# A hybrid layer on one core: a 20th ring slot, one adaLN accumulator instead of two, and other orders of the loads and the weight rounding

## The chip, the cores and the metric

The kernel runs on one core of a Trainium2 chip. The metric is the device time of one execution in microseconds (us). Before the change three runs took 653.33, 655.2 and 656.99 us; their median is 655.2 us.

## The reference

The layer takes x (256 tokens of 1024 values, float32) and a conditioning vector c. Cut to what matters:

```python
mod = silu(c) @ w_ada + b_ada                       # six sections of 1024 columns
shift1, scale1, gate1, shift2, scale2, gate2 = split(mod, 6)
hn   = rms_norm(x, g1) * (1 + scale1) + shift1
proj = hn @ w_in                                    # 3592 columns
q_m, k_m, v_m, o_m, gates(8), q_a, k_a, v_a = split(proj)
q_m, k_m = split(silu(causal_conv4(concat(q_m, k_m))))
h_m = rms_norm(mlstm(q_m, k_m, v_m, gates)) * sigmoid(o_m)     # 4 heads x 128
h_a = causal_attention(q_a, k_a, v_a)                          # 8 heads x 64
x   = x + gate1 * (concat(h_m, h_a) @ w_out)
hn2 = rms_norm(x, g2) * (1 + scale2) + shift2
ffn = top-1 of 4 groups, top-2 of its 8 experts:
      sum of weight * ((silu(hn2 @ w_gate[e]) * (hn2 @ w_up[e])) @ w_down[e])
out = rms_norm(x + gate2 * ffn, g_final)
```

The weights of all 32 experts (three matrices of 1024 by 512 each) are read, 6 loads of 1 MiB per expert.

## The kernel before, in words

*Weights and the ring.* Every large weight comes in loads of about 1 MiB on the SP queue into a pool `ring` of `RING = 19` slots of `SLOT = 4 * 520` float32 columns. A slot is free again when its last reader is done, so the SP queue waits for that reader before it issues the load that reuses the slot. `x`, its normalised and transposed copies and the activations `hH`, `hL` lie in ring slots too. The names of loads are: `B0` to `B3` (tile `wb`) for section 1 of adaLN (scale1), `A00` to `A53` (tile `wa`) for two k-chunks each of sections 0, 2, 3, 4, 5, then `ga0` to `om1` (tiles `wi_ga`, `wi_ka`, ...) for four k-chunks each of a 512-column group of `w_in`, and `W0` to `W3` (`wo`) for `w_out`. The string `LOADS` gives their order on SP. Behind them come the experts (`load_expert`, L1206: `we` for gate and up, `wd` for down).

*The projections.* There are 72 steps: seven column groups in the order ga, ka, va, qm, km, vm, om with eight k-chunks each are steps 0 to 55; `w_out` is steps 56 to 71. A float32 product is made of three products in a faster format: in `split` (L390) ACT rounds a weight chunk to `wh` (L398) and DVE or POOL makes the residual `wl` (L399; POOL for the steps in `ON_POOL_L`). `step` (L407) then issues the matmuls of `wh` with `hH`, of `wh` with `hL` and of `wl` with `hH` (L432 where the result is wanted transposed, L403 to L405 elsewhere). The four buffers `NB = 4` of `wh` and `wl` let the rounding run some steps ahead. `hH` and `hL` are the rounded activations and their residual, first scaled only (`h_scaled`), for va and later with shift (`h_full`, L467 to L469).

*adaLN.* A section is a vector times a 1024 by 1024 matrix. Section 1 is done on TensorE (`scale1`, L291). In the others DVE multiplies k-chunks by their scalar and sums them into an accumulator `acc` of 128 by 1024 (`ada_dve`, L219: all eight chunks of section 2, six in sections 0, 3, 4 and 5), and TensorE does the remaining chunks and sums the accumulator over its partitions (`ada_mm`, L227). The accumulators are two buffers of the pool `wk`; `y4`, the results of four experts that wait for their outer product, have the same tag and so the same buffers. `shift_cols` (L453) turns section 0 into the columns `sh`, through the table `dd`. `shift_bias` (L457) multiplies them with the weights of q and k.

*What sets the order.* TensorE's order is written out by hand from `PLAN`, a table that gives each piece of side work a step before which it stands (`ad5:64` is section 5's matmuls before step 64). The other engines' orders come from a scheduler, which takes the pieces as `PLAN` places them; `AFTER` adds constraints: `w42>dec0` says that the piece `dec0` is issued behind the rounding of step 42 on the engines that both use. Loads on SP are issued in the order of `LOADS`, each as soon as its slot is free.

*Gates.* The eight gate columns of `w_in` lie beside group ga, whose tiles are 520 columns wide for them; POOL copies them out into `wg` (`gate_w`, L573). The scan over tokens runs between `gate_cum` (`pf`, L600) and the decays (`dec0` to `dec3`).

*Experts.* Tokens are gathered per expert by a one-hot matmul (`pair`, L969), then L1094 makes gate and up, L1111 down, `evac_y` (L1116) multiplies by gate2 into `y4`, and after every fourth expert an outer product (`acc_mm`) adds `y4` to the output. An overflow part, entered only where an expert has more than 32 tokens, does the rest in single blocks.

Of the kernel before, what the change touches and what calls it, by code (L numbers as in the profile page):

```python
# [42 lines left out]
PLAN = """
    shb:7 scl:24 hs0:-3 hs1:-3 sb1:1 hs2:1 hs3:1 sb2:3 hs4:3 hs5:3 sb3:4 hs6:4 hs7:4 a00:4 a01:4 a02:6 a03:6 a04:9
    a05:9 a24:20 a25:20 a26:22 a27:23 a44:39 a45:40 a46:41 a47:42 a34:53 a35:54 a36:55 a37:56 a54:62 a55:63 a56:64
    a57:64 ldga0:-3 ldga1:-3 ldA00:-3 ldA01:-3 ldA02:-3 ldA03:-3 ldka0:-3 ldka1:-3 ldva0:-3 ldva1:-3 ldqm0:-3 ldqm1:2
    ldkm0:7 ldkm1:15 ldvm0:12 ldvm1:17 ldA20:-3 ldom0:19 ldom1:20 ldA21:4 ldA22:5 ldA23:5 ldA40:15 ldW2:21 ldW3:37
    ldA41:19 ldA42:19 ldW0:41 ldW1:42 ldA43:21 ldA30:33 ldA31:40 ldA32:41 ldA33:45 ldA50:49 ldA51:51 ldA52:53 ldA53:53
    gw0:5 gw1:6 ad0:11 shc:13 sbq:14 sbk:18 hf0:13 hf1:13 hf2:13 hf3:13 hf4:14 hf5:14 hf6:16 hf7:16 eq0:10 eq1:10
    eq2:10 eq3:10 bq0:17 bq1:17 bq2:17 bq3:17 ek0:20 ek1:18 ek2:18 ek3:18 eva0:24 eva1:24 vm1:33 gp0:18 gp1:20 glog:20  # L50
    gcum:23 grow:26 gcol:33 gs0:26 gs1:26 gs2:26 gs3:27 gs4:27 gs5:27 gs6:28 gs7:28 mo:28 mr:30 dec0:40 dec1:41
    dec2:45 dec3:46 am0:20 ae0:20 ap0:23 av0:25 ae1:20 ap1:24 av1:26 am2:22 ae2:22 ap2:25 av2:26 ae3:22 ap3:26 av3:28
# [20 lines left out]
def tile_hymba_layer(  # L73
# [1057 lines left out]
    def overflow():  # L1131
        n = nc.values_load(nblk_i[0:1, 0:1], min_val=0, max_val=MAXB - 1)
        wb = [wk.tile([P, 512], F32, name=f"wov{i}", tag=("wh", "wl")[i % 2], bufs=NB) for i in range(4)]
        with tc.If(n > 0):
# [251 lines left out]
```

## Time and profile before

| | |
|---|---|
| median of three runs | 655.2 us (653.33 to 656.99) |
| the profiled execution | 657.88 us, span 656.2 us |
| TensorE busy | 522.0 us (80% of the span) |
| VectorE, ScalarE, GpSimd busy | 248.9, 130.8, 73.6 us |
| moved by DMA | 250.43 MB, 380 GB/s over the span |
| longest line | L1094 (gate and up of the experts), 153.7 us of TensorE |

The profiled execution is one of the slower ones of this kernel; its trace gives the durations, the runs give the time. The page cuts the span into 40 slices of 16.4 us. The first eleven or twelve hold the mixer, all later ones the experts. Busy shares are an average over both, so they are read by slice or by stretch.

### The profile page before, as it was taken

The numbers are of one execution on the slowest core, as the hardware profiler recorded it, in microseconds if no ns is written. First come the engines' busy times: TensorE is split into PE (matmuls) and PEld (weight loads), VectorE is DVE, ScalarE is ACT, GpSimd is POOL, SyncE is SP. The second block draws the span as 40 slices with busy tenths as digits, with TensorE's granted clock in tenths as the row PEclk, the third lists the DMA queues.
The fourth block names the chain that finished last, engine by engine and source line by source line (L and its number), as shares of the span: only waits on it lengthen the run. The fifth ranks groups of instructions, "written<-read, shape, count | busy, mean of one in ns | idle before, by whom it ended". The sixth has DMA issues, their size and how long they took to land. (4 is left out here: it accounts for less than half of the span.)

```text
span 656.2 us, 16271 instructions
## 1 busy us (share of the span) xinstructions
PE 522.0 (80%) x7198; PEld 385.4 (59%) x7198; DVE 248.9 (38%) x604; ACT 130.8 (20%) x296; POOL 73.6 (11%) x94
## 2 busy tenths in 40 slices
PE   3879899998998888777677697858876797774885
PEld 3768699786876756545455563635463555452754
DVE  3598799998662322212121212122121312121122
ACT  5343856855440000000000000000000000000023
POOL 7131244724001000000000000000000000000000
PEclk9798999998979999988698866988696977779598
DMA  9999978599969999999999999999999999999982
GB/s 270 380 393 400 395 298 302 212 370 420 379 218 393 415 414 416 415 419 414 417 415 416 416 417 415 416 417 416 418 413 417 415 416 417 417 415 415 416 340 104
DMA packets 56522, 250.43 MB, mean 382 GB/s; under 512 B 4424, under 2 KB 8672, under 8 KB 40064
## 3 DMA queue, kind: packets, MB, share of 16 engines
q1 hardware_dynamic: 55328, 247.51, 94.4%
q0 software_dynamic: 1024, 1.81, 1.1%
q8 instruction: 58, 0.95, 0.6%
q14 instruction: 16, 0.13, 0.1%
q10 hardware_dynamic: 96, 0.03, 0.0%
HBM read 248.27 MB, written 1.06 MB: 380 GB/s over the span
## 5 line engine op out<-in xcount | busy, mean ns | idle before, releaser
L1094 PE MATMUL pgu<-we,xg 128*32 128x128 f32 x4096 | 153.7, 300 | 58.6 <-DMA we<-in_w_expert_up_dram 26.9
L1094 PEld LDWEIGHTS pgu<-we,xg 128*32 128x32 f32 x4096 | 124.0, 120 | 99.8 <-issue 49.7
L1111 PE MATMUL py<-wd,ht 128*32 128x256 f32 x992 | 80.0, 460 | 28.6 <-DVE ht L1105 17.9
L1101 DVE TENSOR_TENSOR hm<-sg,pgu 128x128 f32<-128x128 f32 x32 | 9.2, 288 | 216.6 <-ACT sg L1099 216.6
L1116 DVE TENSOR_TENSOR y<-py,gate 32x256 f32<-32x256 f32 x124 | 52.1, 420 | 92.5 <-PE py L1111 91.2
L1099 ACT ACTIVATE sg<-pgu 128x128 f32<-128x128 f32 x32 | 8.9, 277 | 391.5 <-PE pgu L1094 385.5
L969 PE MATMUL pgx<-oh,xn 128*128 128x64 f32 x512 | 72.3, 303 | 0.8 <-DVE oh L952 0.8
L969 PEld LDWEIGHTS pgx<-oh,xn 128*128 128x128 f32 x512 | 68.1, 215 | 7.0 <-issue 7.0
L1111 PEld LDWEIGHTS py<-wd,ht 128*32 128x32 f32 x992 | 31.3, 125 | 61.1 <-DVE ht L1105 24.3
L225 DVE SCALAR_TENSOR_TENSOR acc<-wa,csil,acc 128x1024 f32<-128x1024 f32 x27 | 38.5, 1426 | 0.2
L912 PE MATMUL acc<-y,owt 128*128 128x512 f32 x64 | 38.0, 722 | 0.1
L959 POOL TENSOR_TENSOR ow<-oh,gg 128x128 f32<-128x128 f32 x16 | 5.9, 394 | 209.4 <-PE pw L1122 183.7
L973 DVE TENSOR_TENSOR xg<-pgx,s 128x256 f32<-128x256 f32 x32 | 12.2, 419 | 37.2 <-PE pgx L969 34.7
L1103 PE MATMUL ph<-ident,hm 128*128 128x128 f32 x32 | 11.1, 346 | 15.9 <-DVE hm L1101 15.1
L1287 POOL MEMSET owz<- 128x1024 f32 x1 | 1.0, 952 | 197.8 <-PE pgu L1094 197.8
L912 PEld LDWEIGHTS acc<-y,owt 128*128 128x128 f32 x64 | 12.9, 226 | 14.0 <-issue 13.5
L1103 PEld LDWEIGHTS ph<-ident,hm 128*128 128x128 f32 x32 | 5.4, 168 | 23.1 <-DVE hm L1101 23.1
L432 PE MATMUL pka<-hH,wl 128*128 128x256 f32 x32 | 9.7, 304 | 5.0 <-DVE wl L399 3.6
L403 PE MATMUL po<-wh,hTH 128*128 128x512 f32 x32 | 13.6, 426 | 0.0
L432 PE MATMUL pga<-hH,wh 128*128 128x256 f32 x32 | 10.4, 324 | 3.9 <-ACT hH L442 3.8
L405 PE MATMUL po<-wh,hTL 128*128 128x512 f32 x32 | 13.2, 413 | 0.0
L404 PE MATMUL po<-wl,hTH 128*128 128x512 f32 x32 | 13.2, 413 | 0.0
(365 smaller groups left out, 764.4 us busy)
## 6 DMA issues: line engine op xcount, KB each, us to landing
we<-in_w_expert_gate_dram SPq DMA_DIRECT2D x64, 1024.0 KB, 20.0
we<-in_w_expert_up_dram SPq DMA_DIRECT2D x64, 1024.0 KB, 20.0
wd<-in_w_expert_down_dram SPq DMA_DIRECT2D x63, 1024.0 KB, 20.0
wa<-in_w_ada_dram SPq DMA_DIRECT2D x20, 1024.0 KB, 11.5
wb<-in_w_ada_dram SPq DMA_DIRECT2D x4, 1024.0 KB, 11.9
wo<-in_w_out_dram SPq DMA_DIRECT2D x4, 1024.0 KB, 7.8
wi_ka<-in_w_in_dram SPq DMA_DIRECT2D x2, 1024.0 KB, 16.2
wi_va<-in_w_in_dram SPq DMA_DIRECT2D x2, 1024.0 KB, 18.2
```

The lines of the kernel that those rows point to most:

```text
L225: V.scalar_tensor_tensor(ACC[sec], w, csil[:, kc:kc + 1], ACC[sec], op0=ALU.mult, op1=ALU.add)
L403: T.matmul(p, aH, bH, start=first, stop=False)
L404: T.matmul(p, aH, bL, start=False, stop=False)
L405: T.matmul(p, aL, bH, start=False, stop=last)
L432: T.matmul(o, a[:, cs], b[:, kc, :], start=(kc == 0 and i == 0 and fb % 2 == 0), stop=(kc == KC - 1 and i == 2), skip_group_check=True)
L912: T.matmul(acc2[tb, h][:, cols], lhsT, rhs, start=start, stop=stop, skip_group_check=True)
L969: T.matmul(pj[j], xn2[:, tb, j, :], oh(tb), start=(tb == 0), stop=(tb == NT - 1))
L973: V.tensor_tensor(xg[:, js], src, s2[:, js].unsqueeze(2).to_broadcast([P, 4, n]), op=ALU.mult)
L1094: T.matmul(pgu[32 * g:32 * g + 32, u * P:(u + 1) * P], xg[:, j, :], wt[:, g * P:(g + 1) * P], start=j == 0 and u == 0, stop=j == KC - 1, s ...
L1103: T.transpose(ph, hm, ident)
L1111: T.matmul(py[32 * g:32 * g + 32, :], ht[:, 32 * f:32 * f + 32], wt[:, c0:c0 + S], start=first, stop=last, skip_group_check=True)
L1116: V.tensor_tensor(y4[r0:r0 + 32, g * S:(g + 1) * S], py[32 * g:32 * g + 32, :], gate2[r0:r0 + 32, g * S:(g + 1) * S], op=ALU.mult)
```

## The change

The ring gets a 20th slot and each slot 24 columns fewer (2056). The room comes from the second accumulator (`acc`, `y4` and the others of that tag now have one buffer), from `dd`, which now lies in columns of `gate2`, from `emt` and `nq`, which now lie in `la` and `lf`, and from the gate columns of group ga, which are loaded by two small DMAs on ACT's queue straight into `wg`. In the final part g_final's row is loaded into row 0 of `gfin`. The overflow part writes its block into a weight slot. `LOADS`, `PLAN`, `AFTER` and `ON_POOL_L` are changed; of `PLAN` two lines are shown.

```diff
-RING = 19
-SLOT = 4 * 520
+RING = 20
+SLOT = 2056
 LOADS = """
-    ga0 B1 B2 ga1 B3 A01 A00 ka0 A02 A03 ka1 va0 va1 qm0 A20 qm1 A21 A22 ...
-    W2 A30 W3 A31 W0 A32 W1 A33 A50 A51 A52 A53
+    ga0 B1 B2 B3 ga1 A01 A00 ka0 A02 ka1 A03 va0 va1 qm0 qm1 A20 A21 A22 ...
+    W2 W3 A30 A31 W0 A32 W1 A33 A50 A51 A52 A53
 PLAN = """
...
-    gcum:23 grow:26 gcol:33 ...
+    gcum:22 grow:26 gcol:33 ...
...
-    ad3:58 sc3:58 ad5:64 tri:40 ... a50:58 a51:59 a52:60 a53:61 ...
+    ad3:58 sc3:58 ad5:68 tri:40 ... a50:56 a51:57 a52:58 a53:59 ...
 AFTER = """
-    w42>dec0 w42>dec1 w47>dec2 w47>dec3
+    w42>dec0 w42>dec1 w47>dec2 w47>dec3 w15>eq0 w8>a03 sb0>w1 sb0>w2
-ON_POOL_L = {2, 5, 8, 11, 14, 17, 20, 23, 26, 27, 31, 33, 37, ...}
+ON_POOL_L = {5, 8, 11, 14, 17, 20, 23, 27, 28, 31, 33, 37, ...}
...
-            acc = ACC[sec] = wk.tile([P, D], F32, name=f"acc{sec}", tag="acc")
+            acc = ACC[sec] = wk.tile([P, D], F32, name=f"acc{sec}", tag="acc", bufs=1)
...
-    dd = const([P, KC, 33], "dd")
+    dd = gate2[:, 0:KC * 33].rearrange("p (j n) -> p j n", j=KC)
...
-    CH = {"ga": (2048, 520, True), "ka": (2568, 512, True), ...
+    CH = {"ga": (2056, 512, True), "ka": (2568, 512, True), ...
...
-    emt = const([P, NT, MH], "emt")
+    emt = la
...
     def gate_w(h):
-        G.tensor_copy(wg[:, 4 * h:4 * h + 4, 0:8], WI["ga", h][:, :, 0:8])
+        A.dma_start(wg[:, 4 * h:4 * h + 4, 0:8], w_in[0, h * 512:(h + 1) * 512, 2048:2056]
+                    .rearrange("(k p) n -> p k n", p=P))
...
-    nq = const([P, NT, MH], "nq")
+    nq = lf
...
-                y1 = wk.tile([P, D], F32, name="y_ov", tag="acc")
-                evac_y(y1, py, 0)
+                for g in range(4):
+                    V.tensor_tensor(wb[g // 2][0:SL, g % 2 * S:(g % 2 + 1) * S], py[32 * g:32 * g + 32, :],
+                                    gate2[0:SL, g * S:(g + 1) * S], op=ALU.mult)
...
-            grow = wk.tile([1, D], F32, name="grow", tag="acc")
-            G.dma_start(grow, g_final.unsqueeze(0))
+            G.dma_start(gfin[0:1, :], g_final.unsqueeze(0))
...
-            y4 = wk.tile([P, D], F32, name=f"y4_{e}", tag="acc")
+            y4 = wk.tile([P, D], F32, name=f"y4_{e}", tag="acc", bufs=1)
```

SP's queue, from the second half of the scale weights on. Before, `wi_ga_248` is ga1 between `wb` loads, and `wi_ka_262` is ka1 behind `wa_3_260`, which is A03:

```order
L286 DMA wb_246<-in_w_ada_dram 128x8x256
L374 DMA wi_ga_248<-in_w_in_dram 128x4x520
L286 DMA wb_250<-in_w_ada_dram 128x8x256
L206 DMA wa_1_252<-in_w_ada_dram 128x2x1024
L206 DMA wa_0_254<-in_w_ada_dram 128x2x1024
L374 DMA wi_ka_256<-in_w_in_dram 128x4x512
L206 DMA wa_2_258<-in_w_ada_dram 128x2x1024
L206 DMA wa_3_260<-in_w_ada_dram 128x2x1024
L374 DMA wi_ka_262<-in_w_in_dram 128x4x512
```

The same place now:

```order
L286 DMA wb_243<-in_w_ada_dram 128x8x256
L286 DMA wb_245<-in_w_ada_dram 128x8x256
L374 DMA wi_ga_247<-in_w_in_dram 128x4x512
L206 DMA wa_1_249<-in_w_ada_dram 128x2x1024
L206 DMA wa_0_251<-in_w_ada_dram 128x2x1024
L374 DMA wi_ka_253<-in_w_in_dram 128x4x512
L206 DMA wa_2_255<-in_w_ada_dram 128x2x1024
L374 DMA wi_ka_257<-in_w_in_dram 128x4x512
L206 DMA wa_3_259<-in_w_ada_dram 128x2x1024
```

ga1 moved behind the last `wb` load, and ka1 ahead of A03.

VectorE in steps 8 to 16, around the shift columns. Before, `wl_577`, `wl_598` and `wl_645` are the residuals of steps 12, 13 and 15:

```order
L225 SCALAR_TENSOR_TENSOR acc_478<-wa_1_252,csil,acc_478 128x1024 x2
L399 TENSOR_TENSOR wl_522<-wi_ka_256,wh_521 128x512
L399 TENSOR_TENSOR wl_541<-wi_ka_256,wh_540 128x512
L225 SCALAR_TENSOR_TENSOR acc_478<-wa_2_258,csil,acc_478 128x1024 x2
L277 TENSOR_TENSOR dd<-pa_613,m_100 128x8x32
L279 TENSOR_REDUCE sh_217<-dd 128x8
L455 COPY shb<-sh_217 128x256
L467 TENSOR_SCALAR xnT<-xnT,s_125,sh_217 128x256 x8
L399 TENSOR_TENSOR wl_577<-wi_ka_262,wh_576 128x512
L399 TENSOR_TENSOR wl_598<-wi_ka_262,wh_597 128x512
L399 TENSOR_TENSOR wl_645<-wi_ka_262,wh_644 128x512
```

Now, where `gate_113` is the table `dd` in its new place and `wl_576`, `wl_594`, `wl_639` are steps 12, 13 and 15:

```order
L399 TENSOR_TENSOR wl_521<-wi_ka_253,wh_520 128x512
L225 SCALAR_TENSOR_TENSOR acc_477<-wa_1_249,csil,acc_477 128x1024
L399 TENSOR_TENSOR wl_540<-wi_ka_253,wh_539 128x512
L225 SCALAR_TENSOR_TENSOR acc_477<-wa_2_255,csil,acc_477 128x1024 x2
L399 TENSOR_TENSOR wl_576<-wi_ka_257,wh_575 128x512
L399 TENSOR_TENSOR wl_594<-wi_ka_257,wh_593 128x512
L277 TENSOR_TENSOR gate_113<-pa_609,m_100 128x8x32
L279 TENSOR_REDUCE sh_216<-gate_113 128x8
L455 COPY shb<-sh_216 128x256
L467 TENSOR_SCALAR xnT<-xnT,s_125,sh_216 128x256 x8
L399 TENSOR_TENSOR wl_639<-wi_ka_257,wh_638 128x512
```

The residuals of steps 12 and 13 moved ahead of the shift columns and of the eight `xnT` operations, that of step 15 stayed behind them.

VectorE in the output projection, from the gating of `hh` on. Before, `wl_1843`, `wl_1875` and `wl_1912` are the residuals of steps 62, 64 and 66:

```order
L703 TENSOR_TENSOR hh<-hh,so_1794 128x512
L248 TENSOR_TENSOR d_1822<-pa_1809,m_100 128x256
L250 TENSOR_REDUCE sh_235<-d_1822 128x8
L737 TENSOR_TENSOR sh_235<-sh_235,colp 128x8
L728 TENSOR_TENSOR wrs<-wst,sh_235 128x8x4
L728 TENSOR_TENSOR wrs<-wst,sh_235 128x8x32
L399 TENSOR_TENSOR wl_1843<-wo_1391,wh_1842 128x512
L739 TENSOR_REDUCE cbs<-wrs 128x36
L728 TENSOR_TENSOR wrs<-wst,s_234 128x8x4
L728 TENSOR_TENSOR wrs<-wst,s_234 128x8x32
L399 TENSOR_TENSOR wl_1875<-wo_1496,wh_1874 128x512
```

The same place now, with `acc_1775` the accumulator of section 5 and `wl_1842`, `wl_1874` the residuals of steps 62 and 64:

```order
L704 TENSOR_TENSOR hh<-hh,so_1793 128x512
L223 TENSOR_SCALAR acc_1775<-wa_0_1549,csil 128x1024
L248 TENSOR_TENSOR d_1821<-pa_1808,m_100 128x256
L225 SCALAR_TENSOR_TENSOR acc_1775<-wa_0_1549,csil,acc_1775 128x1024
L250 TENSOR_REDUCE sh_232<-d_1821 128x8
L399 TENSOR_TENSOR wl_1842<-wo_930,wh_1841 128x512
L225 SCALAR_TENSOR_TENSOR acc_1775<-wa_1_1607,csil,acc_1775 128x1024
L738 TENSOR_TENSOR sh_232<-sh_232,colp 128x8
L399 TENSOR_TENSOR wl_1874<-wo_1454,wh_1873 128x512
L719 SCALAR_TENSOR_TENSOR hTL<-ht_1867,col,hTH 128x256
L225 SCALAR_TENSOR_TENSOR acc_1775<-wa_1_1607,csil,acc_1775 128x1024
L729 TENSOR_TENSOR wrs<-wst,sh_232 128x8x4
```

Section 5's six operations stand between the last residuals of the output projection, whose place before was ahead of all of this, where section 3's six stand now.

## Rows read from the trace of the kernel before

**Rows 1.** The page, 40 slices of the span: share (tenths) and rate of the DMA engines.

```profile
DMA  9999978599969999999999999999999999999982
GB/s 270 380 393 400 395 298 302 212 370 420 379 218 393 415 414 416 415 419 414 417 415 416 416 417 415 416 417 416 418 413 417 415 416 417 417 415 415 416 340 104
```

**Rows 2.** The chain that ended last: start us, us, what it spent them on.

```profile
623.51 21.05 DMA wd<-in_w_expert_down_dram
```

**Rows 3.** Timeline of SP, 181 to 196: start us, us, engine, line, operation.

```profile
181.80 3.91 SPq L1216 DMA_DIRECT2D wd<-in_w_expert_down_dram  x2
195.22 0.34 SPq L1211 DMA_DIRECT2D we<-in_w_expert_gate_dram  x1
```

**Rows 4.** Waits of SP's queue, 168 to 206: us in total, times, longest.

```profile
SPq L1211 <- PE pgu L1094: 12.2, 6, 9.4
```

**Rows 5.** Windows: us, busy PE, PEld, DVE, ACT, POOL, clock, DMA share, GB/s.

```profile
188.00:192.00 4.00, 4.00 (x21) 4.00 (x20) 0.98 (x3) 0.00 (x0) 0.00 (x0) 0.50 0.61 242
192.00:196.00 4.00, 4.00 (x61) 3.76 (x63) 2.58 (x15) 1.06 (x3) 0.00 (x0) 0.50 0.01 2
```

**Rows 6.** Waits of TensorE, 120 to 172.

```profile
PE ht L715 <- DVE hh L703: 2.0, 2, 1.3
PE pm L675 <- DVE st L665: 0.6, 1, 0.6
```

**Rows 7.** Waits of TensorE, 36 to 60.

```profile
PE pka L432 <- DVE wl L399: 3.6, 1, 3.6
PE pka L432 <- POOL wl L399: 1.4, 1, 1.4
```

**Rows 8.** Timeline of VectorE, 45 to 51.

```profile
45.39 3.62 DVE L467 TENSOR_SCALAR xnT<-xnT,s,sh 128x256 f32<-128x256 f32 x8
48.94 1.88 DVE L399 TENSOR_TENSOR wl<-wi_ka,wh 128x512 fp32r<-128x512 f32 x3
```

**Rows 9.** Windows behind three waits of TensorE.

```profile
48.00:52.00 4.00, 2.33 (x16) 2.33 (x17) 4.00 (x11) 1.17 (x3) 0.00 (x0) 0.88 1.04 399
52.00:56.00 4.00, 4.00 (x73) 3.52 (x73) 2.45 (x4) 0.94 (x2) 1.27 (x1) 0.69 1.04 393
156.00:164.00 8.00, 7.63 (x45) 5.69 (x49) 6.64 (x17) 3.46 (x7) 1.75 (x1) 0.79 1.01 417
```

**Rows 10.** The tile of the ka weights, 0 to 60: its two loads.

```profile
DMA to landing us min/median/max: 14.3/16.2/18.1
```

**Rows 11.** Timeline of SP, 21 to 28: the two ka loads.

```profile
21.07 0.63 SPq L374 DMA_DIRECT2D wi_ka<-in_w_in_dram  x1
...
25.84 2.52 SPq L374 DMA_DIRECT2D wi_ka<-in_w_in_dram  x1
```

**Rows 12.** Timeline of TensorE, 30 to 60: steps 4, 8, the shift product, 11, bias, 16.

```profile
30.93 0.39 PE L432 MATMUL pga<-hH,wh 128*128 128x256 f32 x1
...
36.72 0.28 PE L432 MATMUL pka<-hH,wh 128*128 128x256 f32 x1
...
42.69 1.07 PE L238 MATMUL pa<-wa,csb 128*32 128x256 f32 x16
44.12 0.39 PE L432 MATMUL pka<-hH,wh 128*128 128x256 f32 x1
...
53.53 2.40 PE L461 MATMUL pbs<-wi_ga,shb 128*32 128x128 f32 x64
...
58.80 0.39 PE L403 MATMUL pva<-wh,hH 128*128 128x512 f32 x1
```

**Rows 13.** The page, DMA queues: ACT's queue with packets, MB, share.

```profile
q10 hardware_dynamic: 96, 0.03, 0.0%
```

**Rows 14.** VectorE by line, 132 to 146: count, busy, mean ns, idle before.

```profile
L225 DVE SCALAR_TENSOR_TENSOR acc<-wa,csil,acc 128x1024 f32<-128x1024 f32 x5 | 7.0, 1404 | 0.0
```

**Rows 15.** Waits of VectorE, 156.5 to 172.5.

```profile
DVE wl L399 <- ACT wh L398: 4.4, 5, 1.8
```

**Rows 16.** Timeline of VectorE at 140: one accumulation.

```profile
140.21 1.92 DVE L225 SCALAR_TENSOR_TENSOR acc<-wa,csil,acc 128x1024 f32<-128x1024 f32 x1
```

More of the change, by code (lines that the diff above doesn't have):

```diff
@@ L35 @@
 MAXB = S * 2 // SL
-RING = 19
-SLOT = 4 * 520
+RING = 20
+SLOT = 2056
 LOADS = """
-    ga0 B1 B2 ga1 B3 A01 A00 ka0 A02 A03 ka1 va0 va1 qm0 A20 qm1 A21 A22 A23 km0 vm0 km1 A40 vm1 om0 A41 A42 om1 A43
-    W2 A30 W3 A31 W0 A32 W1 A33 A50 A51 A52 A53
+    ga0 B1 B2 B3 ga1 A01 A00 ka0 A02 ka1 A03 va0 va1 qm0 qm1 A20 A21 A22 A23 km0 vm0 km1 A40 vm1 om0 A41 A42 om1 A43
+    W2 W3 A30 A31 W0 A32 W1 A33 A50 A51 A52 A53
 """.split()
@@ L44 @@
     shb:7 scl:24 hs0:-3 hs1:-3 sb1:1 hs2:1 hs3:1 sb2:3 hs4:3 hs5:3 sb3:4 hs6:4 hs7:4 a00:4 a01:4 a02:6 a03:6 a04:9
[L45 to L51, printed above, removed]
+    a05:9 a24:20 a25:20 a26:22 a27:23 a44:39 a45:40 a46:41 a47:42 a34:53 a35:54 a36:55 a37:56 a54:60 a55:61 a56:62
+    a57:62 ldga0:-3 ldga1:-3 ldA00:-3 ldA01:-3 ldA02:-3 ldA03:-3 ldka0:-3 ldka1:-3 ldva0:-3 ldva1:-3 ldqm0:-3 ldqm1:-3
+    ldkm0:5 ldkm1:10 ldvm0:7 ldvm1:15 ldA20:-3 ldom0:17 ldom1:19 ldA21:2 ldA22:4 ldA23:5 ldA40:15 ldW2:21 ldW3:21
+    ldA41:19 ldA42:19 ldW0:40 ldW1:41 ldA43:20 ldA30:33 ldA31:37 ldA32:41 ldA33:42 ldA50:45 ldA51:49 ldA52:51 ldA53:53
+    gw0:5 gw1:6 ad0:11 shc:13 sbq:14 sbk:18 hf0:13 hf1:13 hf2:13 hf3:13 hf4:14 hf5:14 hf6:16 hf7:16 eq0:13 eq1:13
+    eq2:13 eq3:13 bq0:16 bq1:16 bq2:16 bq3:16 ek0:20 ek1:18 ek2:18 ek3:18 eva0:24 eva1:24 vm1:33 gp0:18 gp1:20 glog:20
+    gcum:22 grow:26 gcol:33 gs0:26 gs1:26 gs2:26 gs3:27 gs4:27 gs5:27 gs6:28 gs7:28 mo:28 mr:30 dec0:40 dec1:41
     dec2:45 dec3:46 am0:20 ae0:20 ap0:23 av0:25 ae1:20 ap1:24 av1:26 am2:22 ae2:22 ap2:25 av2:26 ae3:22 ap3:26 av3:28
@@ L57 @@
     mp0:54 mp1:55 ht4:36 ht5:34 ht6:38 ht7:39 ht0:61 ht1:62 ht2:63 ht3:63 row2:16 row5:60 ad2:26 pb1:53 ad4:50 sc2:50
-    ad3:58 sc3:58 ad5:64 tri:40 a20:18 a21:19 a22:20 a23:21 a40:38 a41:39 a42:40 a43:41 a30:51 a31:52 a32:53 a33:54
-    a50:58 a51:59 a52:60 a53:61 xta:55 xu0:71 xu1:70 xT0:71 xT1:71 lb:73 xq0:71 xq1:70 sqt:70 ldB1:-3 ldB2:-3 ldB3:-3
-    pb2:72 pd1:30 pd2:70
+    ad3:58 sc3:58 ad5:68 tri:40 a20:18 a21:19 a22:20 a23:21 a40:38 a41:39 a42:40 a43:41 a30:51 a31:52 a32:53 a33:54
+    a50:56 a51:57 a52:58 a53:59 xta:56 xu0:71 xu1:70 xT0:71 xT1:71 lb:73 xq0:71 xq1:70 sqt:70 ldB1:-3 ldB2:-3 ldB3:-3
+    pb2:72 pd1:30 pd2:71
 """
 AFTER = """
-    w42>dec0 w42>dec1 w47>dec2 w47>dec3
+    w42>dec0 w42>dec1 w47>dec2 w47>dec3 w15>eq0 w8>a03 sb0>w1 sb0>w2
 """.split()
 PLAN = {k: int(v) for k, v in (w.split(":") for w in PLAN.split())}
-ON_POOL_L = {2, 5, 8, 11, 14, 17, 20, 23, 26, 27, 31, 33, 37, 38, 39, 41, 43, 44, 45, 46, 51, 53, 54, 57, 60, 61, 63, 65}
+ON_POOL_L = {5, 8, 11, 14, 17, 20, 23, 27, 28, 31, 33, 37, 38, 39, 41, 43, 44, 45, 46, 51, 53, 54, 57, 60, 61, 63, 65}
 ON_DVE_H = set()
@@ L362, in tile_hymba_layer @@
     WI, PJ, WS = {}, {}, {}
-    CH = {"ga": (2048, 520, True), "ka": (2568, 512, True), "va": (3080, 512, False), "qm": (0, 512, True),
+    CH = {"ga": (2056, 512, True), "ka": (2568, 512, True), "va": (3080, 512, False), "qm": (0, 512, True),
           "km": (512, 512, True), "vm": (1024, 512, False), "om": (1536, 512, False)}
@@ L1201, in overflow @@
                     for h in range(2):
-                        acc_mm(tb, h, owt[:, tb * P:(tb + 1) * P], y1[0:SL, h * 512:(h + 1) * 512])
+                        acc_mm(tb, h, owt[:, tb * P:(tb + 1) * P], wb[h][0:SL, :])
     WT = {}
@@ L1243, in tile_hymba_layer @@
                 p = bank(f"pgf{h}")
-                T.matmul(p, ones[0:1, :], grow[:, h * 512:(h + 1) * 512], start=True, stop=True)
+                T.matmul(p, ones[0:1, :], gfin[0:1, h * 512:(h + 1) * 512], start=True, stop=True)
                 A.activation(gfin[:, h * 512:(h + 1) * 512], p, AF.Copy)
```

## The prediction, made before the change was run

> **What bounds the kernel now.** I read the page first: its forty slices show the DMA engines busy nearly everywhere, at 415 to 418 GB/s from the fourteenth slice on, with holes only in the first twelve [rows 1]. The chain that ended last says the same of the end: it waits 21.05 us for the last expert's down weights, to 644.6, and only then comes the last arithmetic [rows 2]. So the time is the moment from which the load stream never stops again, plus what is left to load, plus a tail that no part of the change touches (656.2 minus 644.6 is 11.6 us, and 657.88 minus 656.2, that is 1.7 us, around the span).
>
> That moment is in the SP queue's timeline: expert loads go out until 181.80 (two, to 185.7), then none until 195.22 [rows 3]. The queue's waits name the reason: 9.4 us for the matmuls of the first expert [rows 4]. All 19 slots are taken, one by the normalised activations and 18 by the weights of experts 0 to 2. The windows show the hole: 242 GB/s in 188 to 192, 2 GB/s in 192 to 196, DMA share 0.61 and 0.01, so about 0.39 x 4 + 0.99 x 4 = 5.5 us without a transfer [rows 5]. From 196 on the stream is bound by its rate alone; one load is 1.049 MB, at 416 GB/s 2.52 us. I call 195.2 T0. Everything before counts only by what it does to T0 and to the number of loads done by then; the lower digits in the sixth to eighth slice cost nothing by themselves.
>
> T0 itself is set by TensorE. Between 56 and 185 its waits are few: the largest in 120 to 172 are 2.0 and 0.6 us [rows 6]. Earlier there are two, in 36 to 60: 3.6 us for a residual `wl` made on DVE and 1.4 us for one made on POOL [rows 7].
>
> **The change part by part.**
>
> *The slot.* With 20 slots a 19th expert load is out before T0. It needs 2.52 us and the hole has 5.5, so after T0 one load fewer is left: -2.5 us. It cannot be more; it is 0 if the extra slot is not filled by T0, since the accumulators of sections 3 and 5 now hold their weight slots longer. I take -2.5: the slot emptied last in both kernels is that of x, at 185, and only the 19th load waits for it.
>
> *The early loads and DVE's order (T0's first term).* Today DVE does eight `xnT` operations, 3.62 us from 45.39, before the three `wl` of steps 12, 13 and 15 at 48.94 [rows 8]; PE waits 3.6 us for the first. The wait is paid twice, as the granted clock then falls: 0.88 in 48 to 52 and 0.69 in 52 to 56, which is 0.12 x 4 + 0.31 x 4 = 1.7 us of matmul time [rows 9]. In the new order `wl` of steps 12 and 13 stand ahead of the shift columns. With the POOL wait, 3.6 + 1.4 + 1.7 = 6.7 us could go.
>
> What is late next: the load of A03, which now comes behind ka1. The two ka loads land at 21.07 + 14.3 = 35.4 and 25.84 + 18.1 = 43.9, three loads apart, so 2.85 us each [rows 10, 11]. A03 then lands at 43.9 instead of 41.1, and PE's shift product (42.69 to 44.12 today with its accumulator part) cannot start before [rows 12]. I add 1.0 us for the two new gate-column loads on ACT's queue: 1,024 pieces of 32 bytes. No row shows such pieces; the nearest are ACT's 96 packets at 0.0%, which is under 0.33 us of the span, so under 3.5 us for 1,024, and from below 0 [rows 13]. The 8 columns dropped from two weight loads are 33 KB, 0.1 us the other way.
>
> By the Trainium skill ("DMA: Bandwidth & Descriptors", section Specifications) transfers under 512 B are handled as read-modify-write, below line rate; no run here shows it. If that doubled the 1.0, A03 would be 1.0 us later and the term below 1.0 us smaller.
>
> Then: A03 at 44.9, the product 1.4 to 46.3; steps 11 to 13 at (36.72 - 30.93)/4 = 1.45 us each, to 50.7; the bias product of q, 2.40 today partly at the low clock, taken 2.0, to 52.7; steps 14 and 15 to 55.6. Step 16 starts at 58.80 today [rows 12]. That is -3.2 us. Against it stands ga1, which now lands a load later, by 2.85 us: DVE's new order puts `wl` of steps 4 and 6 ahead of the third scale chain, so steps 4 to 7 end about 1.9 us later than 36.72. That is swallowed, since step 8 waits 1.4 for POOL today and PE would wait at 43 for A03 anyway. Term: -3.0 us; from below -6.7 (all waits gone), from above +1.5 (ga1's delay stays and the new wait at A03 lowers the clock as the old one did).
>
> *Scores, gates, conv, decay.* The gate sum's matmuls come one step earlier; the logarithm that they wait for stands on ACT between rounded weights of the same steps, so it moves along with PE: 0. `wl` of step 26 goes to DVE and that of 28 to POOL: 0. The scan's row DMA is issued later on POOL, but the decays that read it move later still, behind the conv and SiLU. With section 3's six accumulations gone from DVE between 106 and 128, its conv, SiLU and `wl` 48 come earlier, which should take most of the 0.6 us wait [rows 6]: -0.5. From both sides: -1 and +1.
>
> *One accumulator instead of two.* Section 3's six operations take the place of section 5's at 133 to 145; section 5's wait for the section 3 product (step 58) and go between the last `wl` of the output projection, behind the gating of hh. Six at 1.40 us [rows 14] are 8.4 us in a stretch where DVE is idle for 4.4 us [rows 15]: 4.0 us too much. Queued behind them are `wl` 62 to 71 and the residual adds, and PE waits for those. PE has cover: a `wl` may be a step or two late (1.45 us each) before PE stops, and section 5's product itself moves from step 64 to 68. Going down the new order row by row with those durations I find `wl` 62 and 66 about level with PE and `wl` 71 at the end about 1 us late. Term: +1.0; from below 0, from above +4.0. Gate 2, which comes of that product, is first read behind T0, some 20 us later: 0.
>
> *The rest* (smaller tables, gfin's row written in place, zeros of the last block) lies in the expert stream, where PE waits for weights: 0. Each block's outer product ends long before the next block, 15 us per expert later, writes the single accumulator.
>
> Sum: -2.5 - 3.0 - 0.5 + 1.0 = -5.0 us. Against the profiled execution, 657.88, that is 652.9; that execution lies 2.7 us above the median of the runs shown, so against 655.2 I forecast **650.2 us**. Half a percent, about what a measurement of this kernel tells from no change, is 3.3 us: faster is below 651.9, slower above 658.5.
>
> **The rivals.**
> 1. *Only the slot counts*: what PE gains at 49 it loses again at A03 and behind section 5's operations; T0 stays. For it: PE is busy almost throughout, so each lost cover shows; against it: the removed wait is 3.6 us and certain, its successor shorter. Time 655.2 - 2.5 = 652.7. The same time results if the slot is not filled by T0 while the rest goes as forecast (-2.5): the change then doesn't do what it says.
> 2. *All early waits go*, with the clock: -2.5 - 6.7 = -9.2, 646.0. Against it: A03 behind ka1.
> 3. *Slower: section 5 on the path.* One accumulation took 1.92 us instead of the mean of 1.40, which I put down to POOL beside it [rows 14, 16]. Six are 11.5, less 4.4 idle, 7.1 us that PE waits in steps 62 to 71, and its clock falls as in 156 to 164 today (0.79, 1.7 us [rows 9]): +8.8. With the slot and an early gain of 2.5 it is +3.8, 659.0. It decides from an overflow of about 7 us on. Against it: POOL is busy only 1.75 of 8 us there.
>
> **How the numbers follow.** Forecast 0.55, with its own range 648.0 to 652.5; rival 1, both forms, 0.23; rival 2, 0.12; rival 3, 0.10. Faster by over 0.5%: nearly all of the forecast (0.52) and rival 2, 0.64. Same: rest of the forecast and rival 1, 0.26. Slower: 0.10. The range reaches from rival 2 to short of rival 3, as the unknown costs allow: 646.0 to 656.5.
>
> **What would show it.** Right: 19 expert loads before the long wait of the SP queue; T0 near 192.5; no 3.6 us wait of PE for `wl` at step 12, but one of 1 to 2 us at the shift product near 44; DVE without idle time between 156 and 172, and PE's projection ending within 1 us of its old distance from step 16; tail 11.6 us. Wrong: a second wait of the loads for something other than the first expert; PE stopped over 2 us in the last ten steps; a load rate other than 415 to 418 GB/s after T0, as the slots now start at other addresses (no row speaks for that).

## The result, and the profile after

The changed kernel takes 649.19 us in the median of 8 runs (647.88 to 652.08), the kernel before 656.1 us in 8 runs beside it (653.33 to 659.25). The ratio is 0.9893 with a 95% interval of 0.9864 to 0.9923: 5 to 9 us faster, about 6.9. The forecast was 5.0 us faster, 650.2.

The profiled execution took 649.25 us with a span of 647.4, against 657.88 and 656.2. The 8.8 us between the two spans are read in the order of the prediction. First the page's slices of the DMA engines, which answer to [rows 1]:

```profile
DMA  9999998679989999999999999999999999999983
GB/s 270 377 396 407 395 383 286 211 273 416 419 336 401 417 418 415 418 417 416 417 418 415 417 418 417 418 420 416 418 419 417 417 419 415 419 420 414 417 358 119
```

The stream is the bound as before, and the hole in the twelfth slice is smaller (336 GB/s instead of 218). The timeline of SP (start, us) has one more load ahead of the long wait than [rows 3], the 19th, at 183.51. T0, the moment from which the queue issues loads again behind the first expert, is 191.98 instead of 195.22. The queue's wait for the first expert is 8.1 us where [rows 4] has 9.4:

```profile
183.51 0.34 SPq L1213 DMA_DIRECT2D we<-in_w_expert_gate_dram  x1
191.98 0.34 SPq L1213 DMA_DIRECT2D we<-in_w_expert_up_dram  x1
```
```profile
SPq L1213 <- PE pgu L1095: 14.5, 6, 8.1
```

The early part. TensorE's two waits of [rows 7] are gone; what is left in 36 to 60 is one of 0.7 us, and the granted clock that [rows 9] shows at 0.88 and 0.69 is 1.00 (waits; windows):

```profile
PE pga L432 <- DVE hL L443: 0.7, 1, 0.7
```
```profile
48.00:52.00 4.00, 4.00 (x83) 3.67 (x82) 4.00 (x13) 3.29 (x9) 0.58 (x1) 1.00 1.07 411
52.00:56.00 4.00, 4.00 (x30) 3.78 (x30) 3.93 (x12) 1.88 (x4) 3.17 (x1) 1.00 1.01 402
```

A new wait stands just ahead of that window: TensorE waits 2.3 us for `hH`, and step 8 starts at 38.99, where [rows 12] has 36.72. The prediction had this delay at 1.9 us. The lead is made behind it (timeline of TensorE):

```profile
31.73 0.38 PE L432 MATMUL pga<-hH,wh 128*128 128x256 f32 x1 [2.31 <-ACT hH L442]
...
38.99 0.28 PE L432 MATMUL pka<-hH,wh 128*128 128x256 f32 x1
```

VectorE's timeline shows why the later waits are gone, against [rows 8]: two residuals at 44.71, the eight `xnT` operations only at 48.12. TensorE reaches the shift product at 43.82, where [rows 12] has 42.69, and step 16 at 54.67 instead of 58.80:

```profile
44.71 2.37 DVE L399 TENSOR_TENSOR wl<-wi_ka,wh 128x512 fp32r<-128x512 f32 x2
...
48.12 2.68 DVE L467 TENSOR_SCALAR xnT<-xnT,s,sh 128x256 f32<-128x256 f32 x8
```
```profile
43.82 1.07 PE L238 MATMUL pa<-wa,csb 128*32 128x256 f32 x16
...
54.67 0.39 PE L403 MATMUL pva<-wh,hH 128*128 128x512 f32 x1
```

The late part. TensorE's timeline before, at the first transpose of `hh` and at the transposes of x behind the output projection:

```profile
154.79 0.30 PE L715 MATMUL ht<-ident,hh 128*128 128x128 f32 x1 [0.77 <-DVE hh L703]
...
175.79 1.05 PE L778 MATMUL x1t<-ident,x 128*128 128x128 f32 x8
```

And after:

```profile
151.17 0.30 PE L716 MATMUL ht<-ident,hh 128*128 128x128 f32 x1 [0.79 <-DVE hh L704]
...
173.89 1.12 PE L779 MATMUL x1t<-ident,x 128*128 128x128 f32 x8
```

The lead is 3.6 us at the first and 1.9 us at the second: 1.7 us are lost in the output projection, where section 5's operations now stand. VectorE has no wait at all from 152.6 to 170, where [rows 15] has 4.4 us. Two of TensorE's waits are new beside that for `hh` (2.1 us, 2.0 in [rows 6]):

```profile
PE ht L716 <- DVE hh L704: 2.1, 2, 1.3
...
PE po L405 <- DVE hTL L719: 0.5, 1, 0.5
PE po L404 <- DVE wl L399: 0.4, 1, 0.4
```

And a stretch that the prediction did not look at, from the first gather to T0. TensorE's timeline before (gather of 32 matmuls, then the first expert's 128), 12.3 us in all:

```profile
186.87 6.37 PE L969 MATMUL pgx<-oh,xn 128*128 128x64 f32 x32 [0.77 <-DVE oh L952]
...
193.22 5.93 PE L1094 MATMUL pgu<-we,xg 128*32 128x128 f32 x128
```

And after, 10.7 us:

```profile
185.03 4.97 PE L970 MATMUL pgx<-oh,xn 128*128 128x64 f32 x32 [0.77 <-DVE oh L953]
...
189.99 5.71 PE L1095 MATMUL pgu<-we,xg 128*32 128x128 f32 x128
```

Both run at a granted clock of 0.5, which is the lower level, 1.2 GHz (0.50 in 188 to 196 in [rows 5], and the same after until 192). So the lead of 1.9 us became a T0 that is 3.2 us earlier: 1.4 us came from a clock that stood a little less long at its lower level. That is a difference between two executions; nothing in the change was shown to cause it.

The profiled spans then add up so: 1.9 (TensorE up to the gather), 1.4 (clock behind it), 2.5 (the 19th load), 1.3 (the rate of the stream, below), 0.4 (tail, 636.20 to 647.4 after) make 7.5 of 8.8 us. The profiled execution of the kernel before lies 1.8 us above its median and that of the changed kernel at its median, so the sum is one of two executions and not of the medians. The remaining 1.3 lie in the first ten loads behind T0, where one load of the kernel before landed 1.5 us late; I did not settle that.

### The profile page after: what moved, and what is told of

Read it like the earlier page. It is cut to its first block, busy times and chain, and to the rows that moved or that the text cites. A ratio compares the mean times of both kernels' runs of the same rounds, so it can differ in the third digit from the quotient of the medians.

```text
span 647.4 us, 16295 instructions
## 1 busy us (share of the span) xinstructions
PE 513.7 (79%) x7198; PEld 379.9 (59%) x7198; DVE 248.7 (38%) x605; ACT 131.9 (20%) x297; POOL 69.4 (11%) x91
## 3 DMA queue, kind: packets, MB, share of 16 engines
q0 software_dynamic: 1024, 1.81, 1.0%
## 5 line engine op out<-in xcount | busy, mean ns | idle before, releaser
L1095 PE MATMUL pgu<-we,xg 128*32 128x128 f32 x4096 | 155.8, 304 | 55.6 <-DMA we<-in_w_expert_gate_dram 25.9
L1095 PEld LDWEIGHTS pgu<-we,xg 128*32 128x32 f32 x4096 | 126.4, 122 | 94.9 <-issue 42.0
L1112 PE MATMUL py<-wd,ht 128*32 128x256 f32 x992 | 78.7, 449 | 29.5 <-DVE ht L1106 15.1
L970 PE MATMUL pgx<-oh,xn 128*128 128x64 f32 x512 | 68.2, 293 | 0.8 <-DVE oh L953 0.8
L970 PEld LDWEIGHTS pgx<-oh,xn 128*128 128x128 f32 x512 | 64.5, 206 | 6.6 <-issue 6.6
L913 PE MATMUL acc<-y,owt 128*128 128x512 f32 x64 | 35.0, 671 | 0.1
L1106 DVE COPY ht<-ph 128x128 f32<-128x128 f32 x32 | 9.3, 289 | 11.2 <-PE ph L1104 11.2
```

Of the source, the lines that this page charges most:

```text
L913: T.matmul(acc2[tb, h][:, cols], lhsT, rhs, start=start, stop=stop, skip_group_check=True)
L970: T.matmul(pj[j], xn2[:, tb, j, :], oh(tb), start=(tb == 0), stop=(tb == NT - 1))
L1095: T.matmul(pgu[32 * g:32 * g + 32, u * P:(u + 1) * P], xg[:, j, :], wt[:, g * P:(g + 1) * P], start=j == 0 and u == 0, stop=j == KC - 1, s ...
L1112: T.matmul(py[32 * g:32 * g + 32, :], ht[:, 32 * f:32 * f + 32], wt[:, c0:c0 + S], start=first, stop=last, skip_group_check=True)
```

## The experiments

**One slot fewer, by the constant.**

```diff
-RING = 20
+RING = 19
```

> The changed kernel with 19 slots instead of 20, all orders as changed. Theory A (the time is the moment T0 at which the first expert's matmuls free slots, plus 2.52 us for each load not yet out): 18 expert loads before the long wait, T0 unchanged at about 192, time 2.5 us above the changed kernel, 651.7. Rival B (the 20th slot only shortens a hole that the stream fills anyway): as the changed kernel within 0.5 us, 649.2. Rival C (the slot is the whole gain): as the kernel before, 656.

Measured: 671.03 us (669.01 to 673.26), ratio to the kernel before 1.0217 [1.0181, 1.0252]. All three theories fell. The profile shows the early part: TensorE waits 18.4 us for the residual of the first scaled activations, since VectorE's order now has section 0's first accumulation, which waits for its weights, ahead of it (waits of TensorE 15 to 60; VectorE's timeline). These weights land no later than before (32.02, in the changed kernel 32.64), and there the same residual is made at 16.97, ahead of them:

```profile
PE pga L432 <- DVE hL L443: 18.4, 2, 17.6
```
```profile
32.05 0.75 DVE L223 TENSOR_SCALAR acc<-wa,csil 128x1024 f32<-128x1024 f32 x1 [14.89 <-DMA wa<-in_w_ada_dram]
...
34.22 0.88 DVE L443 SCALAR_TENSOR_TENSOR hL<-xnT,s,hH 128x256 fp32r<-128x256 f32 x2
```

With nothing but the number of slots changed the scheduler gave VectorE another order. So this run measures an order and not a slot.

**Two slots fewer.** The same with `RING = 18`.

> The same with 18 slots. Theory A: 17 expert loads before the long wait, another 2.5 us, 654.2, if no slot is missing earlier; where the earlier loads of the mixer also come late, more. Rival B: 649.2 to 650. Rival C: well above the kernel before, over 659.

Measured: 683.85 us (681.37 to 686.97), ratio 1.0421 [1.038, 1.0462]: above every time that was expected but that of rival C. T0 is at 217.03 against 213.71 with 19 slots. VectorE's order is a third one, with three accumulations ahead of that residual instead of two, and the stream stops a second time, 20.6 us ahead of its last two loads. It says as little on the slot.

**A slot taken away with the order kept.**

```diff
+        if e == 3:
+            held = slot("held")
+            nc.sync.dma_start(held[0:1, 0:256], g_final[0:256].unsqueeze(0))
+        if e == 24:
+            V.tensor_copy(held[0:1, 256:512], held[0:1, 0:256])
         load_until(e)
```

> The changed kernel in which one slot, the one that x frees, is given to a dummy tile ahead of expert 3's first load and kept until expert 24. The order on TensorE, ScalarE and GpSimd is that of the changed kernel, VectorE has one tiny copy more at expert 24. Theory A (each load that is out before T0 is worth its 2.52 us): 18 loads before the long wait, T0 unchanged at 192.0, time 649.2 + 2.5 = 651.7. Rival B (the hole closes anyway): 649.2. Rival G (what the kernel with 19 slots lost, 22 us, is the price of the missing slot itself and not of VectorE's other order): 660 or more.

Measured: 650.5 us (649.7 to 654.2), ratio 0.9918 [0.989, 0.9946]. Where the changed kernel issues its 19th load, the dummy row goes out, and the 19th load waits until 192.66 (timeline of SP):

```profile
183.69 0.31 SPq L1236 DMA_DIRECT2D held<-in_g_final_dram  x1
192.66 0.36 SPq L1213 DMA_DIRECT2D we<-in_w_expert_gate_dram  x1
```

T0 is 0.68 us later than in the changed kernel and the profiled span 3.2 us longer, so by this pair of profiles the slot itself is worth 2.5 us. The medians differ by 1.3, within the spread of these runs. The slot is not held as long as the expectation says: the copy that frees it ran at 216.9 us, at expert 2 and not 24. It was missing at T0, which is what counts here. Rival G fell: the 22 us were the order.

**The resources without the orders.** `LOADS`, `PLAN`, `AFTER` and `ON_POOL_L` as before, the rest of the change as it is.

> The changed kernel with the load order, the plan, the extra constraints and the set of residuals on POOL of the kernel before: only the slot, the single accumulator, the small tables and the gate columns are changed. Theory A: the 3.6 us wait of TensorE at step 12 is there again, T0 back near 195.2, 19 loads before it: 2.5 us under the kernel before, 653.6. Rival B: 656. Rival C: all of the gain, 649 to 650. Rival D (the single accumulator costs what the orders were changed to win back): above 656.

Measured: 663.99 us (662.96 to 667.91), ratio 1.0127 [1.0088, 1.0166]. Rival D holds, and theory A's price for this kernel was wrong by 10 us. T0 is 207.40 although 19 loads are out. TensorE's largest wait is the mechanism of the prediction's third rival, section 5's product before step 64 (timeline of TensorE):

```profile
177.70 1.08 PE L238 MATMUL pa<-acc,ones 128*32 128x256 f32 x8 [5.62 <-DVE acc L225]
```

This wait and the lower clock behind it are about a third of the loss on TensorE. Against the changed kernel it is 5.5 us late at step 16 (60.13), 11.3 at the first matmul of `w_out` (152.94), behind a wait of 2.8 us in the mLSTM part, and 17.6 at the transposes of x (191.44). The early wait for `wl` at step 12 is there again, with 2.4 us.

**Section 5's product back at step 64.**

```diff
-ad5:68
+ad5:64
```

> The changed kernel with section 5's matmuls ahead of step 64 again instead of step 68. Theory A (the single accumulator puts section 5's six operations into the output projection, and only the later step keeps TensorE from waiting for them): TensorE waits about 4 to 5 us for acc, its clock falls behind the wait, T0 6 to 8 us later, time 655 to 657. Rival H (the operations are not on the path): 649.2.

Measured: 653.77 us (652.33 to 658.55), ratio 0.9981 [0.9953, 1.0008], 4.6 us above the changed kernel. The wait is 5.5 us and the clock falls behind it (a matmul of 0.40 us takes 0.63):

```profile
166.30 1.08 PE L238 MATMUL pa<-acc,ones 128*32 128x256 f32 x8 [5.54 <-DVE acc L225]
...
168.34 0.63 PE L405 MATMUL po<-wh,hTL 128*128 128x512 f32 x1
...
171.52 0.40 PE L405 MATMUL po<-wh,hTL 128*128 128x512 f32 x1
```

Step 70's weights are rounded 7.9 us later, as forecast, but T0 is only 4.1 us later (196.09): in this execution the clock stayed at 1.0 from the gather on. At the gather the delay is 6.2 us (191.22 against 185.03). The later step is thus what keeps TensorE from waiting for the single accumulator.

**ka1 behind A03 again.**

```diff
-    ga0 B1 B2 B3 ga1 A01 A00 ka0 A02 ka1 A03 ...
+    ga0 B1 B2 B3 ga1 A01 A00 ka0 A02 A03 ka1 ...
```

> The changed kernel with one pair of loads swapped back, A03 ahead of ka1. VectorE then has the residuals of steps 12 and 13 behind seven of the eight xnT operations, as before. Theory A (this is where the early gain comes from): TensorE waits 2.4 to 3.6 us for wl at step 12 and its clock falls behind it, step 18 starts 3 to 4 us later than in the changed kernel, T0 near 195, time 652 to 653. Rival F (the order of these loads is worth nothing, because TensorE makes it up later): 649.2.

Measured: 655.21 us (651.49 to 655.93), ratio 0.9975 [0.9952, 0.9998]. VectorE has the residual of step 12 behind seven `xnT` operations, TensorE waits 3.3 us for it, and the clock falls (waits of TensorE 36 to 60; VectorE's timeline; window):

```profile
PE pka L432 <- DVE wl L399: 3.3, 1, 3.3
```
```profile
46.88 3.30 DVE L467 TENSOR_SCALAR xnT<-xnT,s,sh 128x256 f32<-128x256 f32 x7
50.11 0.68 DVE L399 TENSOR_TENSOR wl<-wi_ka,wh 128x512 fp32r<-128x512 f32 x1
```
```profile
52.00:56.00 4.00, 4.00 (x48) 3.87 (x51) 2.59 (x7) 1.80 (x4) 0.10 (x1) 0.63 1.04 411
```

Step 8 starts only 0.2 us later than in the changed kernel (39.22), step 18 5.3 us later, T0 5.6 us later (197.59); the median is 6.0 us higher. Swapping two loads back takes nearly all of the gain.

**Two pairs of loads in their old order.** The expectation speaks of three pairs and names four. The edit swaps two, ga1 with B3 and A03 with ka1; A20 and A30 stay where the changed kernel has them.

```diff
-    ga0 B1 B2 B3 ga1 A01 A00 ka0 A02 ka1 A03 ...
+    ga0 B1 B2 ga1 B3 A01 A00 ka0 A02 A03 ka1 ...
```

> The changed kernel with three pairs of loads in their old order (ga1 before B3, A03 before ka1, A20 before qm1, A30 before W3). Theory A (what counts is VectorE's order, residuals of steps 12 and 13 ahead of the eight xnT operations): ka1 lands near 43.9, TensorE waits 1 to 2 us there instead of 3.6, T0 1.0 to 1.5 later, 650.5. Rival E (the swap of ka1 and A03 is what removes the wait): T0 back near 195, 652.4. Rival F (load order is worth nothing): 649.2.

Measured: 653.62 us (650.05 to 657.63), ratio 0.996 [0.9932, 0.9989]; the runs spread too far to say more than "later than the changed kernel". ka1 is about as late as in the run above (it lands at 43.52, there at 44.40, in the changed kernel at 41.06), but the scheduler left the residuals of steps 12 and 13 ahead of `xnT`:

```profile
48.09 0.69 DVE L399 TENSOR_TENSOR wl<-wi_ka,wh 128x512 fp32r<-128x512 f32 x1
...
49.03 0.69 DVE L399 TENSOR_TENSOR wl<-wi_ka,wh 128x512 fp32r<-128x512 f32 x1
...
50.94 2.67 DVE L467 TENSOR_SCALAR xnT<-xnT,s,sh 128x256 f32<-128x256 f32 x8
```

No wait for `wl` shows, step 18 starts 2.0 us later instead of 5.3, and T0 is 1.4 us later (193.37). The 2.0 us are not ka1's: step 8, ahead of its weights, already starts 2.35 us later than in the changed kernel (41.34 against 38.99), behind a longer wait for `hH` and a lower clock (waits of TensorE 20 to 36; window):

```profile
PE pga L432 <- ACT hH L442: 3.9, 1, 3.9
```
```profile
28.00:32.00 4.00, 4.00 (x78) 3.69 (x78) 0.96 (x3) 0.63 (x1) 1.28 (x1) 0.64 1.02 400
```

Both runs have ka1 late, and the wait at step 12 is only in the one where VectorE has `xnT` first. So the wait follows VectorE's order. What a late ka1 would cost with the new order and no delay ahead of it, no run shows, nor whether ga1's place or the clock made the 2.35 us.

**The gate sum one step later.**

```diff
-gcum:22
+gcum:23
```

> The changed kernel with the gate sum's matmuls (pf) one step later, where they stood before. Theory A (the 1.1 us that TensorE waits for the logarithm in the changed kernel is lost on the path to T0): that wait gone, T0 about 1 us earlier, time 648.2. Rival I (the scan behind it then comes late, or the wait comes back at another place): 649.2 or above.

Measured: 649.41 us (648.05 to 653.37), ratio 0.9906 [0.9874, 0.9939]: rival I by the time. The wait of 1.1 us for the logarithm is gone, and the one at the scores is 1.3 us instead of 0.8. TensorE gains 0.5 us over the stretch: it enters it 0.9 us later than in the changed kernel, since the clock was at its lower level from 32 to 37 in this execution, and leaves it 0.4 us later. T0 is 1.8 us earlier all the same (190.20), because the clock was 1.0 from the gather on (waits, and timeline of TensorE, to be read against the changed kernel's 4.97 and 5.71):

```profile
PE sc L519 <- ACT PT L542: 1.3, 1, 1.3
```
```profile
185.33 3.76 PE L970 MATMUL pgx<-oh,xn 128*128 128x64 f32 x32 [0.77 <-DVE oh L953]
...
189.06 3.70 PE L1095 MATMUL pgu<-we,xg 128*32 128x128 f32 x128
```

**A product moved into the gaps ahead of the gather.**

```diff
+        acc2[1, 1] = bank("acc211", tag="pj")
+        acc_mm(1, 1, ident, x1[:, 1, 512:768], start=True, cols=slice(0, 256))
         T.matmul(pp[:, 0, :], tri_b, am2[:, 0, :], start=True, stop=True)
...
         T.matmul(pp[:, 1, :], ones_b, am2[:, 0, :], start=False, stop=True)
+        acc_mm(1, 1, ident, x1[:, 1, 768:1024], cols=slice(256, 512))
...
-        if e == 1:
-            acc_init(1, 1)
```

> The changed kernel in which the first product of the fourth output accumulator (x1 into its bank), which stands behind expert 1's start, is cut in two halves and moved into the two gaps of 0.5 and 0.8 us that TensorE has in the routing, ahead of the first gather. Theory K (the granted clock of 0.5 behind these gaps in some executions makes the gather and the first expert's matmuls take 10.7 us instead of 7.5, and splits the run times): with the gaps filled the clock stays at 1.0 there, T0 near 190, time 1.5 to 3 us under the changed kernel, 646.2 to 647.7, with less spread. Rival L (the clock falls there whatever stands in the gaps): T0 and time as in the changed kernel, 649.2, or 0.3 above for the later gather.

Measured: 646.36 us (646.21 to 648.21), ratio 0.9852 [0.9822, 0.9882]. It beats both kernels, by 2.8 us the changed one. But the edit does less than the expectation says. In the changed kernel the product in question does not stand behind expert 1's start: all four accumulators' first products, two matmuls each, stand ahead of the routing's matmuls (`pp`):

```profile
179.72 3.68 PE L913 MATMUL acc<-x,ident 128*128 128x512 f32 x8
183.90 0.19 PE L1042 MATMUL pp<-am,cmask 128*128 128x32 bf16 x1 [0.50 <-DVE am L1040]
```

The edit takes half of one product away from there and puts it behind `pp`. So the first gap grows from 0.50 to 0.92 us, and only the second shrinks, from 0.77 to 0.25. The gather and the first expert take 7.5 us, and T0 is 189.87; the gather itself starts no earlier (185.00 against 185.03):

```profile
183.87 0.19 PE L1044 MATMUL pp<-am,cmask 128*128 128x32 bf16 x1 [0.92 <-DVE am L1040]
...
184.08 0.68 PE L913 MATMUL acc<-x,ident 128*128 128x256 f32 x2
185.00 3.76 PE L970 MATMUL pgx<-oh,xn 128*128 128x64 f32 x32 [0.25 <-DVE oh L953]
...
188.73 3.70 PE L1098 MATMUL pgu<-we,xg 128*32 128x128 f32 x128
```

**The same edit in the kernel before.** The edit just shown, made in the kernel before.

> The kernel before with the same two halves of the fourth accumulator's first product moved into the gaps of the routing, nothing else. Theory K: the clock stays at 1.0 from the first gather to T0, T0 near 192.5 instead of 195.2 and 196.5, time near 653, and the two groups of run times (near 654.5 and 658.5) become one. The difference to the changed kernel with the same edit (646.36) is then what the change is worth without the clock: 3.2 us of T0, 2.5 of the slot and 1.2 of the rate, 6 to 7 us. Rival L: times as before, near 656, in two groups.

Measured: 654.41 us (653.34 to 659.63), ratio 0.9994 [0.9964, 1.0024]; the two groups of run times are still there. The profiled execution is one of the upper group (659.63), with the clock at its lower level behind the gaps, which are 0.92 and 0.24 us here too:

```profile
190.47 5.59 PE L969 MATMUL pgx<-oh,xn 128*128 128x64 f32 x32 [0.24 <-DVE oh L952]
...
196.04 5.08 PE L1097 MATMUL pgu<-we,xg 128*32 128x128 f32 x128
```

So theory K is right in what the clock costs (10.7 us against 7.5), and its remedy was tested only in part: closing the second gap does not keep the clock up by itself, and a kernel with both gaps closed was not run. Why the six runs of the changed kernel with this edit lie within 2 us, and those of the kernel before with it in two groups, stays open. For the same reason the 8.1 us between the two medians are not the price of the change without the clock.

**The kernel before, a second profile.**

> The kernel before, a second profile. Theory K: where the time is near 654, the granted clock in the last 8 us ahead of T0 is 1.0 and T0 is 3 to 4 us under 195.2; where it is near 658, the clock is 0.5 there and T0 near 195. Rival M (the runs differ by the rate of the expert stream): T0 near 195 in either, the time of one load 2.547 us instead of 2.555.

Measured: 657.64 us in one run; T0 at 196.48, gather and first expert 5.64 and 5.02 us, again at the lower clock. It is again one of the upper group, so it does not show what the lower group looks like in this kernel. The 14 profiled executions together speak for the clock and do not prove it. Of the eight at the lower clock, 657.88, 657.64, 659.63, 652.37 and 673.26 are high among the runs of their kernels, and 655.21, 649.25 and 683.51 in the middle. Of the six with 7.5 us, four are at the low end (652.62, 650.1, 648.05, 646.32), 664.28, of the run with the old orders, is in the middle, and 674.8 is the only run of its kernel. Rival M fell as far as this run can tell: T0 moved with the clock, and the rate is that of the first profile.

**The slot's size alone.**

```diff
-SLOT = 2056
+SLOT = 4 * 520
```

in the kernel with 19 slots; the order on every engine is the same as there.

> The changed kernel with 19 slots of 2080 columns, all orders those of the kernel with 19 slots of 2056 columns. Theory R (the slots' place in memory sets the rate of the expert stream): one load takes 2.555 us between loads 28 and 188, as in both profiles of the kernel before. Rival S (the rate varies from run to run): 2.545 to 2.550 as with 2056 columns.

Measured: 674.8 us in one run. Both kernels' expert 10 and expert 30, first load of each (timeline of SP; 120 loads lie between the two rows). With 2056 columns:

```profile
307.66 0.57 SPq L1213 DMA_DIRECT2D we<-in_w_expert_gate_dram  x1
...
611.82 0.57 SPq L1213 DMA_DIRECT2D we<-in_w_expert_gate_dram  x1
```

With 2080:

```profile
307.44 0.51 SPq L1213 DMA_DIRECT2D we<-in_w_expert_gate_dram  x1
...
613.05 0.53 SPq L1213 DMA_DIRECT2D we<-in_w_expert_gate_dram  x1
```

That is 304.2 against 305.6 us, or 2.535 and 2.547 us a load; the levels in the expectation are higher, the difference is of the size expected. Theory R is borne out: over the same loads the four profiles with 2080 columns took 305.5 to 305.8 us, the ten with 2056 took 304.2 to 305.2. With the size of the slots the place of all that lies behind the ring moves too, so the runs do not tell the two apart. On 170 loads it is 1.3 us between the kernels before and after (305.5 and 304.6).

## Why the prediction was right, point by point

*The bound and T0.* Right, with one exception. In the runs with the same load rate the profiled spans follow T0 and the loads left: 21.7 us of T0 and one load of 2.5 make the 24.1 us more of the kernel with 19 slots; 5.6 us of T0 and 6.0 of span for ka1 behind A03. With 18 slots the span is 34.4 us longer, and T0 and two loads make only 30.1 of it: there the stream stops once more near its end.

*The slot, -2.5.* Right: 19 loads ahead of T0, and 2.5 us by the profile of the run that takes the slot away (1.3 by the medians). That the change's slot could not be undone by its constant was not foreseen.

*The early part, -3.0.* The mechanism was right, the size too small: step 16 starts 4.1 us earlier, and so does step 18. The wait at the shift product, which I put at 1 to 2 us, did not come: A03 landed at 43.69, TensorE was busy until then and took the product at 43.82. The 1.0 us added for the two gate-column loads was too much. They landed at 18.55 and 20.36, and A03 not later than the 43.9 worked out without them. The page now has, where [rows 13] has 96 packets:

```profile
q10 hardware_dynamic: 1152, 0.07, 0.2%
```

0.2% of 647 us is 1.3 us of all engines' time for 1,056 packets more, where 33 KB at 416 GB/s would be 0.1. It does not show in the large loads: the one in A03's place landed at 43.52 to 44.40 in three profiles with these pieces and at 43.94 in the one without. By the Trainium skill ("DMA: Bandwidth & Descriptors", section Specifications) transfers under 512 B are read, modified and written; the share agrees with small pieces being dear, and says nothing on how.

*Scores, gates, decay, -0.5.* Wrong in sign, +0.5. The lead of 4.1 us at step 18 is 3.6 at the transposes of `hh`, after 2.4 in between. The wait of 0.6 us that was to go fell to 0.3. But the step for the logarithm, which the prediction put at 0 because ACT would move along with TensorE, cost a wait of 1.1 us, and moving the sum back gained 0.5 us on TensorE, which no median shows.

*One accumulator, +1.0.* Mis-sized: +1.7, within the bounds of 0 to 4. The step where the product stands decides it, and the run at step 64 has the prediction's third rival nearly to the letter (5.5 us of wait and a lower clock).

*The sum.* -3.0, -0.5 and +1.0 were to be -2.5 on TensorE; measured are -4.1, +0.5 and +1.7, so -1.9 up to the gather. Two terms were missing that both helped: the clock between the gather and T0 (-1.4 in these two profiles; over the 14 profiled executions the stretch takes 7.5 to 12.3 us) and the rate of the stream with other slot addresses (-1.3). The prediction had named the rate among what would make it wrong and given it nothing. So the time came out 1 us under the forecast, and the gain 2 us larger than forecast; 0.9 of these 2 us are the kernel before, whose median is 656.1 in 8 runs and was 655.2 in three.

That T0 came within 0.5 us of its forecast (191.98 against 192.5) is in part luck: the early part gave 1.1 us more than forecast and the two late terms 1.7 us less, and the clock, which had no term, made up the rest. The mechanisms that the forecast rests on, the slot and the order of VectorE around step 12, held; with these and the late losses alone the profiled gain is 4.4 us (1.9 and 2.5), near the 5.0 of the forecast.

*The signs.* The 19 loads, T0, the missing wait at step 12, VectorE without a wait in the output projection and the tail (11.2 us) came as named. Three did not: the wait at the shift product; the distance from step 16 to the transposes of x, which was to stay within 1 us and grew by 2.2 (117.0 to 119.2); and the rate behind T0, up to 420 GB/s in the slices where 418 was the upper end.

## What to carry to other kernels

Where a scheduler orders the engines, a pool's size and a load's place in a list are inputs of that order: to price a slot, take it away where the order stays, and compare the orders before the times. A kernel that is bound by a load stream is priced by two numbers, the moment from which the stream no longer stops and the loads then left; a saved wait counts only by what it does to these. And the last microseconds ahead of that moment deserve their own look at the granted clock: here a stretch at half speed cost 3.2 us, about as much as the removed wait of 3.6 us gained. Last, read in the trace of an experiment whether its edit did what it was meant to: three here (the held slot, the pairs of loads, the gaps) did something else.

## What the runs showed of the hardware

- Behind two waits of TensorE of 0.50 and 0.77 us (0.92 and 0.25 in two kernels) the granted clock fell to 0.5 in 8 of 14 profiled executions and stayed at 1.0 in the other 6, of nearly the same program: gather and first expert took 10.7 us (12.3 in one) or 7.5. In one set of 17 runs of the kernel before the times stand in two groups, 653.1 to 655.5 and 658.0 to 658.7; in other sets some runs lie between. That the clock makes these groups fits the profiles and is not shown.
- The expert stream ran about 0.3% faster into slots of 8,224 bytes per partition than into slots of 8,320. The cause is open.
- 1,024 pieces of 32 bytes took 0.2% of the DMA engines' span, and no delay of a large load shows.
